# Experts of a mixture: gate and up products with the tokens as the stationary operand, weights split and read unit by unit, modulated rows stored

## The chip, the core and the metric

One core of a Trainium2 chip runs the whole program. The metric is the device time of one execution in microseconds; lower is better. TensorE (PE, its weight loads PEld), VectorE (DVE), ScalarE (ACT), GpSimd (POOL) and SyncE (SP, which here only issues DMAs) run their own instruction queues in order and wait for one another on semaphores.

## What is computed

Two blocks of two layers each on 1024 tokens of width 1024, in float32. The first block (gated delta rule and gated linear attention) is not touched. Each layer of the second block is attention, a residual layer norm, a modulation, a mixture of 32 experts of which each token takes 2, and another residual layer norm:

```python
x = layer_norm_2(DEEPNORM_ALPHA_2 * x + (1 + g1) * y, ln_g[i, 0], ln_b[i, 0])
h = x * (1 + sc2) + sh2
y = hierarchical_moe(h, ...)
x = layer_norm_2(DEEPNORM_ALPHA_2 * x + (1 + g2) * y, ln_g[i, 1], ln_b[i, 1])
# hierarchical_moe: for each expert e, on the rows routed to it
return (jax.nn.silu(xb @ w_gate[e]) * (xb @ w_up[e])) @ w_down[e]
```

`w_gate[e]` and `w_up[e]` are [1024, 512], `w_down[e]` is [512, 1024]; together 6 MB an expert. With this case's inputs, worked out from the reference, the fullest expert has 109 tokens in the first layer and 145 in the second, where the next has 101.

## The kernel before

SBUF is an arena of 47 units of [128, 1024] float32 (512 KB each); PSUM is eight banks of [128, 512]. The program is written as chains (generators) that emit instructions and yield; `Flow.run` picks the next chain by priority and by rough estimates of the engines' times, so one fixed order of instructions for each engine comes out. Every instruction goes through one helper, so the profile gives line 72 to nearly all; shapes and tiles tell them apart.

A float32 product can be made in two ways. As plain float32, TensorE gets one matmul, which stands in the trace as two instructions. As float32r, `split` (line 441) first makes two halves of 12 significant bits: ScalarE copies the value to the high half, VectorE subtracts it from the value for the low half. Three matmuls then give the product: high by high, high by low, low by high. A float32r matmul is one instruction.

A layer's experts run in `moe_experts` (line 2609), at most two open at a time, each a chain `expert` (line 2536):

- `gather` (line 2600): GpSimd clears a unit and fetches the expert's tokens, up to PLACES = 120 rows, from DRAM by an indirect DMA; two experts ahead.
- `turn` (line 564): TensorE turns the rows into eight [128, 120] columns; ScalarE and VectorE take four each out of PSUM, and multiply and shift them by the modulation (`cols`) on the way.
- gate and up: for each of four blocks f of 128 channels, eight plain float32 matmuls with a [128, 128] piece of the weight stationary and the 120 tokens moving. The result has channels on partitions, as the down product needs it.
- ScalarE's silu, VectorE's product and a split; then down: 24 float32r matmuls, the 120 tokens stationary and the weight's halves moving, 512 wide, for two halves n of the width; each half times gate and gain on VectorE, then GpSimd adds the rows to Y in DRAM by an indirect DMA. The last expert's outcome is kept back instead (`hold`).

`Experts` (line 2475) loads the weights ahead on SP, matrix by matrix, each as four units: at most `limit` = 2 matrices at first, 5 later. Gate and up units are read as two pieces of 2 KB for each partition, down units as one of 4 KB. The chain `split` makes the halves of the down matrix's four units; a matrix's units are given back together, at its end.

An expert with more than PLACES tokens gets further blocks in `moe_extra` (line 2666), a loop on the device before the others, in which `Direct` loads the weights for the block; nothing else runs beside it. One such block runs here, in the second layer.

Ahead of the experts, `out_proj_ln` (line 1518) makes the attention's output product tile by tile (eight of 128 tokens). Each tile is normalised in `post` of `moe_front` (line 2293), which also makes the router's logits; `Rows.put` (class at line 1471) then multiplies by ALPHA times gain and adds ALPHA times bias, both on VectorE, and writes the result twice, to x_mid, from which the experts gather, and to Y, to which they add. After the last two tiles `route` counts places; the gathers wait for it. In this stage `Rows.tile` also puts two GpSimd operations of [128, 1024] on each tile that comes in.

Of the kernel before, what the change touches and what calls it, by code (L numbers as in the profile page):

```python
# [30 lines left out]
# Each chain is a generator that emits instructions and yields where its next TensorE work has to wait. Rough  # L31
# estimates of the engines' times say which chain goes on: the first in priority that would not hold TensorE up.
# [27 lines left out]


class Engine:
    """An engine's instructions, each with its estimated time added to the flow's clocks."""
# [51 lines left out]
class Flow:  # L115
# [15 lines left out]
    def ready(self, eng, outs, ins):  # L131
        """When what an instruction reads and writes may be there."""
# [14 lines left out]
    def lag(self, a, b):  # L147
        """From an instruction's end on engine a to the start of one on b that waits for it."""
# [12 lines left out]
    def last(self, ap):  # L161
        """When an access was last used."""
# [20 lines left out]
    def dma(self, out, in_, after=None):  # L183
        """Returns the time by which it may have arrived; after: an instruction that is to end before."""
# [28 lines left out]
    def rank(self, done, prio):  # L213
        """Another priority for a chain, given what spawn() returned."""
# [38 lines left out]
class Buf:  # L253
    """A unit of an arena, or a run of them."""
# [19 lines left out]
class User:  # L274
    """Who takes units: at most peak at a time. Units that earlier users may still need are kept for them."""
# [5 lines left out]
class Arena:  # L281
    """Units of one size; make(i, n, dt) gives the access to n of them from i on, a tensor of its own if fresh."""
# [34 lines left out]
    def now(self, n=1, dt=F32, user=None):  # L317
        """Units that are sure to be free."""
# [30 lines left out]
def rep(ap, n):  # L349
    """A [P, x] access seen as [P, n, x], the same for each n."""  # L350
# [3 lines left out]
def spread(ap, n):  # L354
    """A [P, c] access seen as [P, c, n], each value n times."""
# [3 lines left out]
def rows_of(vec, off, n):  # L359
    """A DRAM vector's n elements from off, for each of 128 partitions."""  # L360
# [55 lines left out]
def sm(K, n):  # L416
    """Room for n values per partition."""
# [3 lines left out]
def rsqrt(K, out, x, n):  # L421
    """out = x ** -0.5 on VectorE: a bit-level first guess and three Newton steps. x, out: [128, n]"""
# [18 lines left out]
def split(K, hi, lo, src, scale=None, pool=False):  # L441
    """src = hi + lo exactly, each with the 12 significant bits of float32r; scale: a power of two. """
# [10 lines left out]
class Weights:  # L453
    """Requests (source, units, scale): DRAM [128, units * 1024] accesses; each comes as (hi, lo) buffers."""
# [5 lines left out]
    def ask(self, srcs, shape, scale=None):  # L460
        """srcs: the unit's DRAM accesses, each with the part of the unit (a function of its view) that it fills."""
# [43 lines left out]
def ask_cols(K, w, col, scale=None):  # L505
    """128 columns of a [D, n] weight as [128, 8, 128]."""
# [4 lines left out]
class XT:  # L511
    """A transposed activation in two float32r halves: hi[k], lo[k] [128, S]; ready[t] per tile of 128 tokens."""
# [6 lines left out]
    def take(self, user=None):  # L519
        """Its units, taken by the first who asks."""  # L520
# [21 lines left out]
def gemm_cols(K, X, w, h):  # L542
    """[128 columns of w, 512 tokens] in a bank, three float32r passes."""
# [20 lines left out]
def turn(K, dst, src, cols=None):  # L564
    """dst, src: [128, 8, 128] accesses; dst[:, c] = transposed src[:, c]; cols [128, 16]: a bias and a scale for each c."""
# [49 lines left out]
def columns(K, vecs):  # L615
    """DRAM vectors of D values as columns [128, (vector, k)]."""
# [15 lines left out]
def affine(K, g, b, out, ready, mod=None, n=0):  # L632
    """Columns (bias | scale) of x g + b, or of that times (1 + sc) + sh: columns n + 1 and n of a layer's modulation."""
# [16 lines left out]
def hybrid_params(K, l):  # L650
    """What a layer needs besides its large weights."""
# [25 lines left out]
    # half of the weights: silu(2 y) = y (1 + tanh(y))  # L677
# [22 lines left out]
def softplus_neg(K, out_ln, x):  # L700
    """out_ln = log(1 + exp(-|x|)); x in SBUF."""
# [19 lines left out]
def small_projections(K, P, X, user):  # L721
    """beta, the decays of the delta rule and the log gates of the linear attention."""
# [41 lines left out]
    # as two float32r parts  # L764
# [4 lines left out]
    # log gates: [128 tokens, 8 chunks, 256]  # L769
# [22 lines left out]
def conv_silu(K, P, X, chunk, user, ev):  # L792
    """silu(causal depthwise convolution) of 128 projected channels: [128, S]."""
# [28 lines left out]
def proj(K, X, user, ev, gate=False, scale=1.0):  # L822
    """128 projected channels [128, S]; gate: 2 silu of them."""
# [21 lines left out]
def proj_rows(K, X, user, ev):  # L845
    """256 projected channels of tokens: [128 tokens, 4, 256] twice."""
# [13 lines left out]
class Out:  # L860
    """128 channels of the heads' outcome: [128, S], to DRAM, or for the last ones as two float32r halves."""
# [19 lines left out]
def head_out(K, o, ss, z, gain, dst, user, by=None):  # L881
    """rms norm of o [128 tokens, 8, 128] per token (ss: sums of squares), its gain, times z [128 channels, S]; to DRAM."""
# [23 lines left out]
def chunks_of(d, c0, n):  # L906
    """n chunks from c0, [128, n, 128], in a DRAM tile where a chunk and the blocks on its diagonal keep one distance."""
# [3 lines left out]
def blocks_of(d, c0, n):  # L911
    """The 16 x 16 blocks on the diagonals of n chunks from c0, [8 n, 16, 16]."""
# [3 lines left out]
def solve(K, H, b, kT, g2, sL, D, L, W):  # L916
    """Half b's transposed T = (I + strict(s k k^T . decay))^-1: blocks of 16 by substitution, then merged in twos."""
# [81 lines left out]
def solve_blocks(K, H, W, g2, user):  # L999
    """The inverses of the 64 blocks I + N of 16 x 16, a partition each, a column of N at a time."""  # L1000
# [18 lines left out]
def norms(K, x, ss, r, user):  # L1019
    """Of [128 tokens, 8, 128]: r = 1 / its rows' lengths."""  # L1020
# [9 lines left out]
def delta_head(K, P, l, h, evs, user, prio, dst):  # L1030
    """Keys and queries stay as they are: their lengths go into the factors of the small matrices and of the outcome."""
# [131 lines left out]
    # the outcome's factors: the queries' ones inside of the norm  # L1163
# [8 lines left out]
def gla_level(K, n, q, k, B, user):  # L1172
    """exp of the decays to a middle place of each 2^(n+1) tokens, times k before it and q after it."""
# [14 lines left out]
def head_sums(K, x):  # L1188
    """Of x [128 = 2 heads x 64, S]: the sums over a head's channels, [128 tokens, (head, 8)]."""
# [11 lines left out]
def gla_pair(K, P, l, pr, evs, user, prio, dsts):  # L1201
# [14 lines left out]
    # both heads' sums over their channels  # L1216
# [65 lines left out]
    # neighbours  # L1282
# [17 lines left out]
    # through the state  # L1300
# [62 lines left out]
def hybrid_layer(K, l, P, X, outs, prio):  # L1363
    """Projections, delta rule and linear attention; the gated heads to outs."""
# [45 lines left out]
def load_rows(K, user, vec):  # L1410
    """A DRAM vector of D values on all partitions."""
# [5 lines left out]
def load_wout(K, w, X, user, out, X2, gain=None):  # L1417
    """A [D, D] weight, its columns times 1 + gain, as out[k] = (hi, lo) [128, D], once X is free; then room is kept for X2."""
# [1491 lines left out]
```

## Time and profile before

| | |
|---|---|
| time, three runs | 4336.83, 4337.46, 4349.83 us; median 4337.46 |
| the profiled execution | span 4333.8 us from the first to the last instruction; 3.7 us less than the median run's time |
| PE busy | 4128.3 us, 95% |
| DVE / ACT / POOL busy | 2642.8 / 1778.6 / 818.2 us |
| DMA | 680.59 MB, 157 GB/s on the mean |
| experts of the first layer | about 2055 to 2728 us of the span |
| experts of the second layer | about 3611 to 4284 us, behind the extra block at 3552 to 3606 us |

The page's second part shows the span in 40 slices, a digit for tenths of a slice's time. A table of stretches gives, for each stretch, the busy time of each engine with its number of instructions, the granted TensorE clock as a share of full speed, the mean busy share of the 16 DMA engines and what they moved. A group of instructions lists those of one shape: count, busy time, mean duration of one, idle time before them and who ended it. PE's matmuls overlap in the pipeline: the mean duration of one is longer than the distance from one start to the next, which sets the rate.

### The profile page before, as it was taken

How to read it: one execution, taken by the hardware profiler on the slowest of the kernel's cores; microseconds unless marked ns; L12 is line 12 of the kernel's file. 1: busy time of each engine (PE TensorE's matmuls, PEld its weight loads, DVE VectorE, ACT ScalarE, POOL GpSimd, SP SyncE). 2: the span in 40 equal slices, each digit the busy share in tenths (PEclk: the TensorE clock that was granted, in tenths of full speed). 3: DMA queues.
4: the chain of work that ended last, by engine and by line, in shares of the span. 5: the costliest groups of instructions: out<-in, count | busy, mean ns of one | idle time of the engine just before them, and what ended most of it. 6: DMA issues, size and time to landing. Idle time of an engine off the chain costs nothing. (4 is left out here: it accounts for less than half of the span.)

```text
span 4333.8 us, 71282 instructions
## 1 busy us (share of the span) xinstructions
PE 4128.3 (95%) x28070; PEld 3462.6 (80%) x28070; DVE 2642.8 (61%) x5593; ACT 1778.6 (41%) x3541; POOL 818.2 (19%) x600
## 2 busy tenths in 40 slices
PE   8999899999999999987999999899999978999997
PEld 6878787888887777766999999776776768999995
DVE  7778767776767766586443444656666674444445
ACT  4333335332334444431333333667777513333331
POOL 1111101211213222241122221300010211222212
PEclk9999899999999999988999999999999989999998
DMA  4323232111134333234999997300010357999994
GB/s 150 85 84 95 79 101 82 49 43 51 41 100 142 117 109 109 81 129 176 323 327 328 326 328 259 112 13 18 20 66 20 112 177 245 324 322 328 335 329 146
DMA packets 404775, 680.59 MB, mean 157 GB/s; under 512 B 59893, under 2 KB 190639, under 8 KB 404437
## 3 DMA queue, kind: packets, MB, share of 16 engines
q1 hardware_dynamic: 386004, 642.85, 43.0%
q0 software_dynamic: 18432, 33.15, 3.4%
q8 instruction: 223, 3.65, 0.3%
q14 instruction: 116, 0.94, 0.1%
HBM read 621.66 MB, written 84.02 MB: 163 GB/s over the span
## 5 line engine op out<-in xcount | busy, mean ns | idle before, releaser
L72 PE MATMUL banks<-slot 128*128 128x120 f32 (+7 forms) x23848 | 3659.8, 317 | 31.5 <-ACT slot L72 13.0
L72 PEld LDWEIGHTS banks<-slot 128*128 128x128 f32 (+4 forms) x23848 | 2982.1, 181 | 585.6 <-issue 213.5
L72 DVE TENSOR_TENSOR slot<-slot 128x1024 fp32r<-128x1024 f32 (+15 forms) x1027 | 851.1, 844 | 452.1 <-ACT slot L72 396.0
L72 ACT ACTIVATE slot<-slot 128x1024 fp32r<-128x1024 f32 (+9 forms) x621 | 579.4, 938 | 817.3 <-DMA slot<-in_moe_w_down 363.2
L72 ACT ACTIVATE slot<-banks 128x512 f32<-128x512 f32 (+8 forms) x929 | 444.6, 491 | 750.8 <-PE banks L72 713.9
L72 POOL TENSOR_TENSOR slot<-slot 128x384 f32<-128x384 f32 (+2 forms) x232 | 343.3, 1501 | 1376.3 <-DVE slot L72 344.8
L72 PE MATMUL banks<-c,slot 128*128 128x128 f32 (+4 forms) x3224 | 477.4, 284 | 90.6 <-DVE slot L72 29.7
L72 PEld LDWEIGHTS banks<-c,slot 128*128 128x128 f32 (+3 forms) x3224 | 383.1, 150 | 167.7 <-issue 58.7
L72 ACT ACTIVATE slot<-banks,small 128x120 f32<-128x120 f32 (+1 forms) x400 | 262.7, 682 | 472.0 <-PE banks L72 399.9
L72 DVE TENSOR_TENSOR slot<-slot,banks 128x512 f32<-128x512 f32 (+3 forms) x175 | 114.5, 660 | 475.0 <-PE banks L72 261.2
L72 ACT ACTIVATE slot<-slot,small 128x1024 f32<-128x1024 f32 (+1 forms) x292 | 266.4, 922 | 237.9 <-DVE small L72 231.4
L72 DVE COPY slot<-banks 128x512 f32<-128x512 f32 (+7 forms) x406 | 221.4, 551 | 129.8 <-PE banks L72 99.2
L72 POOL MEMSET slot<- 120x1024 f32 (+2 forms) x70 | 66.4, 954 | 1066.3 <-PE banks L72 847.6
L72 DVE TENSOR_REDUCE small<-banks 128x1 f32<-128x1024 f32 x128 | 156.2, 1223 | 104.5 <-PE banks L72 104.5
L72 POOL DMA_INDIRECT Y<-slot,small x62 | 139.3, 2246 | 261.9 <-DVE slot L72 260.4
L72 DVE TENSOR_TENSOR slot<-banks,slot 64x512 fp32r<-64x512 f32 (+3 forms) x257 | 123.8, 497 | 64.4 <-ACT slot L72 54.3
L72 DVE SCALAR_TENSOR_TENSOR small<-small 128x1 f32<-128x1 f32 (+3 forms) x590 | 131.9, 230 | 12.5
L72 DVE SCALAR_TENSOR_TENSOR slot<-slot,c_act 128x1024 f32<-128x1024 f32 x84 | 119.5, 1424 | 24.8 <-DMA slot<-in_ada_w 24.1
L72 PE MATMUL banks<-small,slot 128*128 128x128 f32 (+1 forms) x576 | 104.5, 296 | 24.1 <-DVE small L72 19.7
L72 PEld LDWEIGHTS banks<-small,slot 128*128 128x128 f32 (+1 forms) x576 | 81.9, 196 | 39.7 <-issue 17.0
L72 DVE SCALAR_TENSOR_TENSOR slot<-banks,cw,slot 128x511 f32<-128x511 f32 (+1 forms) x144 | 106.8, 745 | 6.1 <-ACT slot L72 4.1
L72 DVE SCALAR_TENSOR_TENSOR slot<-banks,small,slot 120x512 f32<-120x512 f32 x128 | 95.4, 745 | 23.3 <-PE banks L72 23.3
(133 smaller groups left out, 1715.1 us busy)
## 6 DMA issues: line engine op xcount, KB each, us to landing
slot<-in_moe_w_down SPq DMA_DIRECT2D x260, 512.0 KB
slot<-in_moe_w_gate SPq DMA_DIRECT2D x260, 512.0 KB
slot<-in_moe_w_up SPq DMA_DIRECT2D x260, 512.0 KB
slot<-in_ada_w SPq DMA_DIRECT2D x96, 512.0 KB
slot<-in_w_in SPq DMA_DIRECT2D x56, 512.0 KB
xb<-slot SPq DMA_DIRECT2D x40, 512.0 KB
slot<-xb SPq DMA_DIRECT2D x24, 512.0 KB
slot<-in_na_w_qkv SPq DMA_DIRECT2D x24, 512.0 KB
```

The source lines that it names most:

```text
L72: r = real(*a, **k)
```

## The change

PLACES becomes 128. Gate and up are turned round: the tokens' columns are stationary ([128, 128] for each of eight pieces k of the depth) and the weight moves, 512 wide. Each unit of gate and up now holds two rows of the weight for each partition, which lie side by side in DRAM, so it is read in one 4 KB piece; the columns of x are picked in the same order (every second one). Of the eight gate and up units of an expert, the first of each matrix stays plain float32 (`PLAIN`); the other six, and down's four, are split, up to six units ahead of their use (`SPLIT`). Units are loaded, counted (`limit` 8, 20, 22 units) and given back one by one. The tokens' columns are split as well. The product's result has tokens on partitions and takes four more transposes ahead of down. Down's two halves run side by side, a unit at a time.

The modulation leaves the expert: `Rows.prepare` makes two more rows on all partitions from gain, bias and modulation (one VectorE and three GpSimd operations of [128, 1024]), and `put` makes the modulated rows with them on VectorE, for x_mid, ahead of the residual rows for Y, whose two operations go from VectorE to GpSimd. Room kept for this stage goes from 37 to 39 units. Comments and docstrings are removed throughout.

```diff
-PLACES = 120  # of an expert, in one go
+PLACES = 128
+PLAIN = (0, 4)
+SPLIT = 6
+def units_of(w, i):
+    return w.rearrange("o (n p j) f -> p (o n) (j f)", n=4, j=2 if i < 2 else 1)
 class Experts:
     def load(self):
...
-                w = K.I[name][self.l][e].rearrange("(k p) f -> p k f", p=128)
-                b, t = yield from load_matrix(K, i, lambda k, n: w[:, k:k + n, :], self.user)
+                w = units_of(K.I[EXPERT_W[u // 4]][self.l][e:e + 1], u // 4)
+                b = yield from K.A.take(self.user)
+                t = K.F.dma(b.f, w[:, u % 4])
+                if u in PLAIN:
+                    K.F.set(self.there[e][u], (b,), t)
                 else:
-                    self.raw.append((b, t))
+                    self.raw.append((e, u, b, t))
     def split(self):
...
+            while not self.raw or self.ahead >= SPLIT:
+                yield lambda: self.raw and self.ahead < SPLIT
+            e, u, b, t = self.raw.pop(0)
+            self.ahead += 1
             yield from K.F.until(t)
+            w = yield from self.halves(b)
+            K.F.set(self.there[e][u], w)
 def expert(...):
-    xT = yield from A.take()
-    turn(K, xT.rows()[:, :, :c], x.rows()[:c], cols)
+    xh, xl = yield from several(A, 2, None, F32R)
+    xf = sm(K, 2 * c)
+    xv = x.f[:c].rearrange("p (n c j) -> p n j c", n=4, j=2)
+    for g in range(2):
+        p = yield from K.banks.take()
+        for j in range(4):
+            T.transpose(p.f[:, j * c:(j + 1) * c], xv[:, 2 * g + j // 2, j % 2], K.ident[:c, :c])
+        if not g:
+            F.scalar.activation(xf.f[:, 0:2 * c], p.f[:, 0:2 * c], AF.Copy)
+        o, m = (0, 4 * c) if g else (2 * c, 2 * c)
+        split(K, xh.r[:, 4 * g * c + o:4 * g * c + o + m], xl.r[:, 4 * g * c + o:4 * g * c + o + m], p.f[:, o:o + m])
...
-        for f in range(4):
-            for k in range(KD):
-                T.matmul(p.f[:, f * c:(f + 1) * c], wv[k // 2][:, k % 2, f * 128:(f + 1) * 128], xT.rows()[:, k, :c],
-                         start=(k == 0), stop=(k == KD - 1))
+        for n in range(4):
+            w = yield from get.next(i, n)
+            for j in range(2):
+                k, s = 2 * n + j, slice(512 * j, 512 * j + 512)
+                if len(w) == 1:
+                    T.matmul(p.f[:c], xf.f[:, j * c:(j + 1) * c], w[0].f[:, s], start=(k == 0), stop=(k == KD - 1))
+                else:
+                    cut = slice(k * c, (k + 1) * c)
+                    product(p.f[:c], xh.r[:, cut], xl.r[:, cut], w, s, k == 0, k == KD - 1)
+            get.done(w)
             yield
...
+    for f in range(4):
+        T.transpose(p.f[:, f * c:(f + 1) * c], a.f[:c, f * 128:(f + 1) * 128], K.ident[:c, :c])
 class Rows:
     def prepare(self, K, user, write=False):
+        if self.mod is not None:
...
+            K.F.vector.tensor_scalar(sc.f, sc.f, 1.0 / ALPHA, 1.0 / ALPHA, op0=ALU.mult, op1=ALU.add)
+            P.tensor_mul(g.f, self.rows[0].f, sc.f)
+            P.tensor_mul(sc.f, self.rows[1].f, sc.f)
+            P.tensor_add(sc.f, sc.f, sh.f)
-    def put(self, K, x, t):
+    def put(self, K, x, t, user):
+            h = yield from K.A.take(user)
+                V.tensor_mul(h.f, x.f, self.rows[2].f)
+                V.tensor_add(h.f, h.f, self.rows[3].f)
+                K.F.dma(self.also[t * 128:(t + 1) * 128, :], h.f)
             if self.early:
-                self.affine(K, x, 2)
+                self.affine(K, x)
-        freed.limit = 5
+        freed.limit = 20
-        W.limit = 5
+        W.limit = 22
```

## Rows read from the trace of the kernel before

**Rows 1.** page, busy tenths in 40 slices of 108 us

```profile
PE   8999899999999999987999999899999978999997
DVE  7778767776767766586443444656666674444445
DMA  4323232111134333234999997300010357999994
```

**Rows 2.** stretch: length, PE, PEld, DVE, ACT, POOL busy, PEclk, DMA, GB/s

```profile
4000.00:4100.00 100.00, 99.85 (x760) 92.80 (x760) 39.47 (x57) 32.10 (x48) 20.16 (x14) 1.00 0.97 332
```

**Rows 3.** chain that ended last, second layer: start, us, what

```profile
3649.13 20.90 PE banks L72 x160
...
4214.59 20.92 PE banks L72 x160
```

**Rows 4.** PE groups, 2302.4 to 2323.3 us: count, busy, mean ns, idle

```profile
L72 PE MATMUL banks<-slot 128*128 128x120 f32 x128 | 15.1, 275 | 0.0
L72 PE MATMUL banks<-slot 128*120 128x512 f32 x24 | 6.3, 403 | 0.0
L72 PE MATMUL banks<-c,slot 120*128 120x120 f32 x8 | 1.1, 266 | 0.0
```

**Rows 5.** PE group of 1983 to 1990 us; two timeline rows

```profile
L72 PE MATMUL banks<-slot 128*128 128x512 f32 x31 | 7.3, 393 | 0.0
...
2728.34 1.88 PE L72 MATMUL banks<-slot,c 128*128 128x512 f32 x4
...
1979.36 1.03 PE L72 MATMUL banks<-c,slot 128*128 128x128 f32 x8
```

**Rows 6.** table of stretches inside one expert's period

```profile
2329.00:2334.00 5.00, 5.00 (x35) 4.48 (x34) 0.79 (x1) 1.66 (x2) 2.05 (x2) 1.00 1.02 418
2334.00:2336.00 2.00, 2.00 (x20) 2.00 (x19) 2.00 (x3) 1.63 (x3) 0.00 (x0) 1.00 1.04 395
2316.00:2320.00 4.00, 4.00 (x39) 4.00 (x38) 2.09 (x2) 0.51 (x1) 2.31 (x1) 1.00 1.01 253
2322.00:2325.00 3.00, 2.97 (x25) 2.65 (x24) 2.21 (x5) 2.04 (x5) 0.00 (x0) 1.00 1.01 322
2325.00:2327.00 2.00, 2.00 (x17) 1.85 (x16) 0.51 (x2) 0.00 (x0) 0.00 (x0) 1.00 0.59 226
```

**Rows 7.** groups by shape, DVE and ACT, 2300 to 2321 us

```profile
L72 DVE TENSOR_TENSOR slot<-slot 128x1024 fp32r<-128x1024 f32 x4 | 4.8, 1219 | 7.6 <-ACT slot L72 7.6
L72 DVE TENSOR_SCALAR slot<-banks,small 128x120 f32<-128x120 f32 x4 | 1.5, 400 | 0.0
L72 DVE SCALAR_TENSOR_TENSOR slot<-banks,small,slot 120x512 f32<-120x512 f32 x2 | 1.5, 745 | 0.0
L72 DVE TENSOR_TENSOR slot<-slot,banks 128x480 f32<-128x480 f32 x1 | 0.7, 655 | 5.2 <-PE banks L72 5.2
...
L72 ACT ACTIVATE slot<-slot 128x1024 fp32r<-128x1024 f32 x4 | 4.2, 1058 | 7.7 <-DMA slot<-in_moe_w_down 7.5 <-ACT slot L72 0.2
L72 ACT ACTIVATE slot<-banks 128x480 f32<-128x480 f32 x1 | 0.6, 571 | 0.1
```

**Rows 8.** timeline, the first layer's norm tiles: start, us, operation, count

```profile
1914.75 16.57 POOL L72 TENSOR_TENSOR slot<-slot 128x1024 f32<-128x1024 f32 x6 [0.19 <-DMA slot<-xb]
...
1924.36 7.17 DVE L72 SCALAR_TENSOR_TENSOR small<-small 128x1 f32<-128x1 f32 x4
...
1942.01 1.50 DVE L72 SCALAR_TENSOR_TENSOR small<-small 128x1 f32<-128x1 f32 x7
```

**Rows 9.** timeline, PE: router's wait; products of the extra block

```profile
2035.20 0.18 PE L72 MATMUL banks<-both,before_b 128*128 128x32 bf16 x1 [8.59 <-DVE both L72]
...
3573.29 16.76 PE L72 MATMUL banks<-slot 128*128 128x120 f32 x126 [1.50 <-DMA slot<-in_moe_w_up]
...
3591.43 5.83 PE L72 MATMUL banks<-slot 128*120 128x512 f32 x24 [1.38 <-ACT slot L72]
```

**Rows 10.** group of the whole run: GpSimd on [128, 1024]

```profile
L72 POOL TENSOR_TENSOR slot<-slot 128x1024 f32<-128x1024 f32 x76 | 182.4, 2403 | 661.1 <-DMA slot<-xb 322.5 <-ACT slot L72 201.9 <-DVE slot L72 91.4
```

More of the change, by code (lines that the diff above doesn't have):

```diff
@@ L1556, in finish @@
         if not after.early:
-            after.put(K, x, t)
+            yield from after.put(K, x, t, user)
         yield
@@ L1560, in finish @@
         if after.early:
-            after.put(K, x, t)
+            yield from after.put(K, x, t, user)
         A.give(x)
@@ L2326, in moe_front @@
     K.banks.give(p)
[L2327 to L2328 removed]
+    K.small.give(c)
     M.there = [Event() for _ in range(NT)]
@@ L2479, in __init__ @@
         self.K, self.l = K, l
-        self.limit, self.out, self.go = 2, 0, Event()
-        self.raw, self.there = [], [[Event() for _ in range(3)] for _ in range(32)]
+        self.limit, self.out, self.ahead, self.go = 8, 0, 0, Event()
+        self.raw, self.there = [], [[Event() for _ in range(12)] for _ in range(32)]
         self.user = K.A.user(5000, 0)
@@ L2486, in load @@
         for e in range(32):
-            for i, (name, kk, n) in enumerate(EXPERT_W):
+            for u in range(12):
                 while self.out >= self.limit:
@@ L2533, in done, with expert @@
         self.out -= 1
-def expert(K, get, tok, gate, gn, cols, rows, Y, x=None, hold=None):
+        if len(bufs) > 1:
+            self.ahead -= 1
+def expert(K, get, tok, gate, gn, rows, Y, x=None, hold=None):
     F, T, V, A = K.F, K.F.tensor, K.F.vector, K.A
@@ L2574, in expert @@
         F.set(hold.near)
+    yield
+    ps = [(yield from K.banks.take()), (yield from K.banks.take())]
+    for f in range(4):
+        w = yield from get.next(2, f)
+        for n in range(2):
+            product(ps[n].f[:c], hh[:, f], hl[:, f], w, slice(n * 512, n * 512 + 512), f == 0, f == 3)
+        get.done(w)
+        if f < 3:
+            yield
     for n in range(2):
         s = slice(n * 512, n * 512 + 512)
-        p = bank(K)
-        for f in range(4):
-            yield
-            T.matmul(p.f[:c], hh[:, f], w[f][0].r[:, s], start=(f == 0), stop=False)
-            T.matmul(p.f[:c], hh[:, f], w[f][1].r[:, s], start=False, stop=False)
-            T.matmul(p.f[:c], hl[:, f], w[f][0].r[:, s], start=False, stop=(f == 3))
-        with F.aside() if n == 0 else ExitStack():
-            V.scalar_tensor_tensor(y.f[:c, s], p.f[:c], gate[:c], gn.f[:c, s], op0=ALU.mult, op1=ALU.mult)
-            K.banks.give(p)
-            if hold is not None:
-                split(K, h[0].r[:c, s], h[1].r[:c, s], y.f[:c, s])
-                F.set(hold.half[n], h)
-    get.done([b for hl in w for b in hl])
+        V.scalar_tensor_tensor(y.f[:c, s], ps[n].f[:c], gate[:c], gn.f[:c, s], op0=ALU.mult, op1=ALU.mult)
+        K.banks.give(ps[n])
+        if hold is not None:
+            split(K, h[0].r[:c, s], h[1].r[:c, s], y.f[:c, s])
+            F.set(hold.half[n], h)
     A.give(hs)
@@ L2606, in gather, with moe_experts @@
     return x
-def moe_experts(K, l, W, R, gn, cols, rows, Y, prio, first, hold, there):
+def moe_experts(K, l, W, R, gn, rows, Y, prio, first, hold, there):
     F = K.F
@@ L2715, in moe_extra @@
         block()
-        for _ in expert(K, Direct(K, l, e), tok, gate[:, 2:3], gn, cols, rows, Y):
+        for _ in expert(K, Direct(K, l, e), tok, gate[:, 2:3], gn, rows, Y):
             pass
@@ L2811, in moe_layer @@
     ln = F.spawn(moe_ln(K, l, Y, last_one.rrows(), hold, there, x_out, N, user, prio + 200), prio + 200)
-    yield from moe_experts(K, l, W, R, gn, M.cols.f, rows.x, Y, prio + 110, first, hold, there)
-    K.small.give(M.cols)
+    yield from moe_experts(K, l, W, R, gn, rows, Y, prio + 110, first, hold, there)
     K.small.give(R.small)
```

109 lines of the change are left out of this document (54 added, 55 removed).

## The prediction

> **What bounds the kernel now.** I read the slices first: where the experts run at their steady pace (slices 20 to 24 and 35 to 39) PE and DMA show nines, and VectorE threes and fours [rows 1]. So two resources are candidates there, and the table of one such stretch says how close they are: PE is busy 99.85 of 100 us at full clock, and the DMA engines 0.97 at 332 GB/s [rows 2]. The chain of waits decides between them. In the second layer it is PE on itself: 28 rows of 160 matmuls each, one per expert, with starts from 3649.13 to 4214.59, which is 27 periods of 20.94 us, and no wait for data between them [rows 3]. PE sets the pace, and the DMA engines, with 0.97 x 20.94 = 20.3 us of work in each period, are only 0.6 us behind. A cure for PE alone would be worth little; the change touches both.
>
> What PE does in a period is 128 instructions of 120 columns for gate and up (64 matmuls of two), 24 of 512 columns for down and 8 transposes, 160 in all [rows 4]. The 128 take some 14.6 of the 20.94 us: a load of 128 stationary columns is paid for only 120 moving ones.
>
> **The change part by part. PE.** Rates at full clock first. 31 float32r matmuls of 512 columns took 7.3 us with a mean duration of 0.39; (7.3 - 0.39) / 30 is a distance of 0.230 us, so the last one's end stands out by 0.16. Four plain float32 instructions of 512 columns took 1.88, so (1.88 - 0.16) / 4 = 0.43 each; eight transposes 1.03, so 0.109 each [rows 5]. After the change an expert has four plain pieces of the depth (two units of two), 4 x 2 x 0.43 = 3.44; twelve split ones, 12 x 3 x 0.230 = 8.28; down, 24 x 0.230 = 5.52; transposes, 12 x 0.109 = 1.31. The sum is 18.55 us against 20.94. The strided stationary operand of the eight transposes of x is not in this trace; its cost lies between nothing and 0.11 each (as much again as a transpose), 0.9 an expert. I take nothing, since it is off the bound below.
>
> **DMA.** The bytes stay: 332 GB/s x 20.94 us = 6.95 MB an expert, of which 12 x 512 KB = 6.29 are weights. Only the pieces change, 2 KB to 4 KB for two thirds of them. Down's 4 KB pieces move at 418 GB/s with the engines full, a stretch nearly all of 2 KB pieces at 395 [rows 6]. That is 6%, far less than a halved count of pieces suggests. Two phases of each period are slower although the engines are just as full: 253 GB/s for 4 us behind the scatter to Y, 322 for 3 us during the gather [rows 6]. I keep both phases as they are, since their slowness comes with the rows that are added and fetched, and put the rest at 418: 4 us for 1.01 MB, 3 us for 0.97 MB, and 4.97 MB / 418 = 11.9 us. The sum is 18.9 us. From below the bound is 6.95 / 418 = 16.6 (the slow phases gone). From above it is 19.7: today's two microseconds at a share of 0.59 [rows 6], where a transfer waits for units, come on top with 0.8. I take 19.1, near the middle sum, because units now come back one by one. So **DMA would set the pace, at 19.1 us**, half a microsecond over PE's sum.
>
> **Splits.** ScalarE and VectorE now make the halves of ten units instead of four. VectorE: ten subtractions of 1.22 are 12.2; x's halves 0.66 and about half of it; the product 0.66; the split ahead of down 0.66; two gated outcomes 1.49; in all 16.0 us. The 1.5 us of modulations go. ScalarE: ten copies of 1.06 and five smaller ones of up to 0.57, some 13 us [rows 7]. Both lie beside PE and fit into 19.1 us, VectorE with 84%. If that cover goes they are the bound (third rival).
>
> Sum of the steady part: 62 periods (64 experts, less the first of each layer) x (19.1 - 20.94) = **-114 us**.
>
> **Ahead of the experts.** For each tile two VectorE operations are replaced by two others of the same shape, and two of 2.4 us go to GpSimd [rows 10]: 16 in each layer. For the first six tiles PE's products cover them. The last two tiles have no cover: PE waits 8.59 us for the router's chain on VectorE [rows 9], and GpSimd's four operations, 9.6 us, now run beside that chain. What that does the trace shows: beside six GpSimd operations (1914.75 to 1931.3) four tiny VectorE operations of [128, 1] took 7.17 us; seven of them took 1.50 with GpSimd idle [rows 8]. So between 0 and 9.6 us a layer; I take 5, as the router's operations are many and some fall between. In `prepare`, three GpSimd operations and one of VectorE (1.2) do the same while attention ends: 0 to 8.4 a layer, I take 2, since other chains give PE work there. Together +14 for both layers. The Trainium skill, SBUF — State Buffer (SBUF: two separate sides), states an exclusive lock: a VectorE operation with two SBUF inputs waits for a whole GpSimd operation that reads SBUF. This trace's 7.17 us agree; by the rule in full these terms would be +36 instead of +14 and the time 4261.
>
> The modulated rows are written ahead of the residual ones, so the gathers don't wait longer; Y is due only at the first scatter, some 40 us later: nothing. SP issues as many weight DMAs as before, one per unit: nothing.
>
> **Edges.** At a layer's start PE can begin with the plain unit, but the next units need splits of 1.2 us each, which at four already ran there: 0 to 3 us, I take 1 a layer. At the end the last expert's extra transposes (0.4) and their copy stand alone: 0 to 2, I take 1. The extra block of the second layer is serial: its products take 16.76 + 5.83 = 22.6 us [rows 9], and 18.6 after; but up to four splits come ahead of PE's use: -5 to +5, I take -2. Together +2.
>
> Sum: -114 + 14 + 2 = -98 us on the profiled span of 4333.8, so 4235.8. That span lies 3.7 us below the median of the three runs, which takes the same difference: **4239 us**.
>
> **The rivals.** *PE's floor is reached.* If the two slow DMA phases shrink with the larger pieces, PE's 18.55 sets the pace: 62 x (18.55 - 20.94) = -148, +16, 4205 us. For it: only 2 KB pieces run in those phases today, so nothing shows how 4 KB ones fare. Against it: the rate of full engines differs by 6% only. The Trainium skill, Perfetto Trace Analysis (DMA Optimizations), says that batching from 2 KB to 4 KB can dramatically improve throughput; that would end here, and this trace's 395 against 418 GB/s don't bear it out.
>
> *The larger pieces gain nothing.* Then the DMA work stays 20.3 us a period: 62 x (20.3 - 20.94) = -40, +16, 4314 us. The row of 418 GB/s speaks against it.
>
> *VectorE's queue sets the pace.* Its queue is in order, and six of its operations for an expert wait for PE (x's two, the product, down's split, two outcomes); the splits of coming units stand behind them. Today that shows as 5.2 us of idle time ahead of the product [rows 7], harmless at 40% load. With 16.0 us of work, waits of 4.2 us a period give 20.2 us and 4337 - 46 + 16 = 4308. Up to six units split ahead, some 8 us of PE work, speak against it.
>
> *Slower, by the same queue.* From waits of 4.9 us on, the period exceeds today's. If each of the six operations waits 1 us, it is 22.0: 62 x 1.06 = +66, +16, 4419 us. For it: one such wait alone is 5.2 today. Against it: such a wait costs PE nothing while units split ahead last, and the change lets six be ahead.
>
> **How the numbers follow.** Forecast, DMA at 19.1: 0.45. PE's floor: 0.20. VectorE's queue at 20.2: 0.15. Pieces without gain: 0.07. Slower by the queue: 0.09. All within 13 us of today, a mixture of these: 0.04. The range takes the first three: its low end is PE's floor with the extra block's best case and the other terms at nothing (-148 - 5), 4184; its high end is the queue's 4308, rounded to 4310. A measurement of this kernel can tell about 0.3%, 13 us: faster 0.45 + 0.20 + 0.15 + 0.07 = 0.87, same 0.04, slower 0.09.
>
> **What would show it.** Right: periods of about 19 us between the scatters to Y, PE with short idle times put down to DMA or to the splits' halves, a DMA share of 0.97 or more at some 365 GB/s (6.95 MB / 19.1), VectorE at 80 to 87%. PE without idle time and a period of 18.6 is the first rival; PE waiting for VectorE with a DMA share under 0.93 is the queue. The router's wait of 8.59 us growing to 12 or more would show GpSimd's operations beside it. The prediction is wrong if the slow DMA phases change their length with the larger pieces, or if VectorE waits longer for PE than the splits ahead cover.

## The result and the profile after

The changed kernel takes 4623.72 us (median of six runs, 4616.56 to 4643.76) where the kernel before took 4340.91: a ratio of 1.0656, 95% interval 1.0633 to 1.068. It is 6.6% slower; the forecast was 2.3% faster.

The profiled execution took 4643.76 us, the longest of the six, with a span of 4641.8 us, 308 more than before. The slices of its page answer to [rows 1]:

```profile
PE   8999999999999999778878789899999868888787
DVE  7778767757676665776656566665576766565667
PEclk9999899999999999778988989999999878989888
DMA  4333241112242332348777776100022267777774
```

Where the experts run (slices 19 to 24 and 34 to 39) PE shows sevens and eights and DMA sevens (one eight), where both had nines, and the granted clock shows more eights than nines, where it had nines nearly throughout. No resource is full any more. A stretch of each kernel, before and then after, as in [rows 2] (length; PE, PEld, DVE, ACT, POOL busy; PEclk; DMA share; GB/s), says the same:

```profile
2200.00:2600.00 400.00, 399.45 (x3056) 372.31 (x3055) 164.71 (x228) 129.78 (x190) 85.24 (x57) 1.00 0.96 329
...
2200.00:2600.00 400.00, 321.83 (x1227) 236.34 (x1228) 240.33 (x249) 190.87 (x236) 66.34 (x45) 0.89 0.76 262
```

The scatters to Y mark the experts and divide the span. Between the starts of the first and the 31st of a layer lie 752.9 and 748.7 us, where 626.4 and 626.0 lay before: +249 us in 60 distances (25.0 instead of 20.9 on the mean; the median is 26.0, since the first and the last of a layer are shorter). From the first bn aggregate of the normalisation stage to the first scatter (in the second layer to the extra block's) the two layers took 370.8 us instead of 325.2: +46. The stretch from the extra block's scatter to the first of the second layer's experts and the tail behind the last scatter are 4 us shorter together. The other 17 us lie ahead of the change, in code that is the same in both (last section). 249 + 46 - 4 + 17 = 308.

What an expert waits for shows in one period. These are timeline rows of after (start, us, engine, operation, count; in brackets the idle time before and what ended it):

```profile
2396.47 1.59 POOL L72 DMA_INDIRECT Y<-slot,small  x1 [0.16 <-DVE slot L72]
...
2405.91 1.23 DVE L72 TENSOR_TENSOR slot<-slot 128x1024 fp32r<-128x1024 f32 x1 [6.59 <-DMA Y<-slot,small]
2407.17 2.00 ACT L72 ACTIVATE slot<-slot 128x1024 fp32r<-128x1024 f32 x2 [8.29 <-DVE slot L72]
...
2410.14 1.12 PE L72 MATMUL banks<-c,slot 128*128 128x128 f32 x4 [5.13 <-DVE slot L72]
...
2411.04 3.62 PE L72 MATMUL banks<-slot,small 128*128 128x512 f32 x4
```

GpSimd starts the scatter at 2396.47. A subtraction that makes a weight's low half is to write into the very unit that the scatter still reads, so VectorE stands for 6.59 us until the scatter lands; the subtraction starts 9.4 us after the scatter. The profile leaves buffer numbers out, so which unit an instruction takes is inferred from who waits for whom; two experiments below put it to the test. Behind it on VectorE's queue stands the product of gate and up; ScalarE waits for VectorE, then PE 5.13 us for that product. PE's clock has dropped when it goes on after these 5.13 us: the granted clock of the next 5 us is 0.50, its lower level, and the four plain float32 instructions take 3.62 us, in [rows 5] 1.88.

```profile
2410.00:2415.00 5.00, 4.87 (x10) 2.70 (x11) 3.97 (x6) 3.91 (x6) 0.00 (x0) 0.50 0.14 57
```

The waits of after from 2200 to 2600 us (who waited for what: us in total, times, longest) put 11 of some 15 periods down to the scatter, and five waits to weights that come late:

```profile
ACT slot L72 <- DVE slot L72: 171.4, 76, 8.8
...
PE banks L72 <- DVE slot L72: 81.3, 16, 5.6
DVE slot L72 <- DMA Y<-slot,small: 72.6, 11, 6.8
...
DVE slot L72 <- DMA slot<-in_moe_w_up: 27.1, 5, 7.1
```

Ahead of the experts the router's row, as in [rows 9], has grown:

```profile
2070.94 0.19 PE L72 MATMUL banks<-both,before_b 128*128 128x32 bf16 x1 [12.77 <-DVE both L72]
```

### The profile page after: what moved, and what is told of

Its sections match the earlier page's. It is cut to its first block, busy times and chain, and to the rows that moved or that the text cites. A ratio compares the mean times of both kernels' runs of the same rounds, so it can differ in the third digit from the quotient of the medians.

```text
span 4641.8 us, 62336 instructions
## 1 busy us (share of the span) xinstructions
PE 4132.4 (89%) x22870; PEld 3207.2 (69%) x22870; DVE 3122.0 (67%) x5851; ACT 2131.4 (46%) x3866; POOL 924.6 (20%) x638
## 5 line engine op out<-in xcount | busy, mean ns | idle before, releaser
L72 PE MATMUL banks<-slot 128*128 128x512 f32 (+8 forms) x17868 | 3356.4, 352 | 41.9 <-DVE slot L72 18.2
L72 PEld LDWEIGHTS banks<-slot 128*128 128x128 f32 (+4 forms) x17868 | 2532.7, 180 | 739.1 <-issue 293.0
L72 DVE TENSOR_TENSOR slot<-slot 128x1024 fp32r<-128x1024 f32 (+14 forms) x1352 | 1316.9, 984 | 674.7 <-DMA Y<-slot,small 265.1
L72 ACT ACTIVATE slot<-slot 128x1024 fp32r<-128x1024 f32 (+5 forms) x946 | 926.8, 1009 | 1132.2 <-DVE slot L72 779.2
L72 PE MATMUL banks<-c,slot 128*128 128x128 f32 (+2 forms) x3484 | 544.8, 296 | 369.8 <-DVE slot L72 303.6
L72 PEld LDWEIGHTS banks<-c,slot 128*128 128x128 f32 (+1 forms) x3484 | 439.9, 163 | 468.1 <-DVE slot L72 313.8
L72 POOL TENSOR_TENSOR slot<-slot 128x384 f32<-128x384 f32 (+3 forms) x270 | 449.1, 1683 | 1433.8 <-DVE slot L72 407.7
L72 PE MATMUL banks<-slot,small 128*128 128x512 f32 (+2 forms) x648 | 353.9, 686 | 16.3 <-ACT small L72 8.6
L72 DVE TENSOR_TENSOR slot<-banks,slot 128x512 fp32r<-128x512 f32 (+6 forms) x452 | 229.3, 538 | 74.5 <-ACT slot L72 63.7
L72 ACT ACTIVATE slot<-banks,small 128x1024 f32<-128x1024 f32 x140 | 156.2, 1117 | 73.3 <-DVE small L72 72.8
```

Of the source, the lines that this page charges most:

```text
L72: r = real(*a, **k)
```

## The experiments

**The unit of the outcome.** The theory: when the planner gives the outcome y back, it takes the scatter to end 4.04 us after its start (1.04 in `pool_cost` and 3.0 in `Engine`), so that a split gets a unit that is still being read. One line tells it a later time (13.04; the expectations call a unit a slot):

```diff
+    F.mark("POOL", F.last(y.f) + 9.0, [], [y.f])
     A.give(y)
```

> The changed kernel with one line added: the planner is told that the slot of an expert's outcome y comes free 9 us later than it had assumed, so that it gives other slots to the next splits; nothing else of the computation or of the queues is edited. Theory (the slot): in the changed kernel one split subtraction on VectorE waits up to 7.4 us per expert for the scatter that still reads its slot, and the product of gate and up and PE stand behind it. Then this wait is gone, the distance between scatters falls from 26.3 us to 18.5 to 20.5 us, and the time falls by 62 x (26.3 - 19.5) = some 360 to 480 us less what DMA then holds up: 4180 to 4350 us. Rival (VectorE's queue by itself: its operations wait for PE's results, whichever slots they use): the distance stays at 25 us or more and the time above 4540 us. Rival (weights arrive late): the same 25 us or more, with VectorE waiting for the weights' transfers instead of the scatter.

4304.59 us, ratio 0.992 (0.9891 to 0.9949): 319 us from one line. The distance is 19.30, constant to 0.03 in the middle of the first layer, and VectorE waits neither for a scatter nor for `in_moe_w_up` any more: the late weights came of the same stall.

```profile
2200.00:2600.00 400.00, 390.14 (x1660) 292.55 (x1659) 310.77 (x332) 256.30 (x312) 92.41 (x61) 1.00 0.98 354
```

PE is at full clock, so the clock of 0.89 in after was a consequence of the stalls. PE was busy for 321.83 / 400 x 26.0 = 20.9 us a period there, with 5.1 idle; here for 18.8 with 0.5 idle. Of the 6.7 us between the periods 4.6 are idle time and 2.1 the clock.

The other way to take the wait away is to take the reader of the unit away.

```diff
-    F.gpsimd.indirect_dma_start(out=Y, ..., compute_op=ALU.add)
```

> The changed kernel without the scatters of the experts' outcomes (the rows are not added; nothing else is edited, the planner is not told of another time). Theory (the slot): a slot that no scatter reads has nothing to wait for, so the distance between the gathers falls from 26.3 us to 18.7 to 19.5 us, as with the slot's correction. Rival (the correction helped because it dealt the slots out in another order): the distance stays above 23 us. What it falls below 19.3 is the scatter's own price on the DMA engines.

The distance between gathers is 19.1 us. Two quite different edits, a later time in the planner and no scatter at all, take the same 7 us away; without the scatter an expert is only 0.2 us shorter than with the later time.

A smaller dose:

```diff
+    F.mark("POOL", F.last(y.f) + 2.0, [], [y.f])
```

> The changed kernel with a smaller dose of the slot's correction: the planner takes the outcome's slot to be free 2 us later than it had assumed (6 us after the scatter's start instead of 4), where the scatter lands 9.3 us after its start (median of the changed kernel). Theory (the slot): the slot goes to a split that VectorE reaches about 2 us later, so the wait of 6.6 us per expert shrinks to 4 to 5 us and the distance between scatters to 23 to 24.5 us, between the 26.1 without and the 19.3 with 9 us. Rival (any other order of the slots would have cured it): 19.3 us. Rival (the wait has another cause): 26 us.

4252.27 us, a distance of 18.55: not the part of the gain that I expected (a period of 23 to 24.5 us), but more than all of it. The same kernel once more:

> The kernel with the slot declared free 2 us later once more, timed: its one run was 4252 us beside 4340 for the kernel before. In that run a weight load, not a split, took the outcome's slot, so SyncE's queue waits for the scatter and VectorE does not, and PE was busy without a gap at 18.55 us an expert, the sum that my prediction had for PE. I expect 4235 to 4265 us, a ratio of 0.975 to 0.985.

4248.98 us, ratio 0.9789 (0.977 to 0.9808). Stretch and PE timeline:

```profile
2200.00:2600.00 400.00, 400.00 (x1728) 306.42 (x1727) 329.90 (x345) 261.72 (x325) 90.89 (x63) 1.00 0.98 365
```

```profile
2353.06 1.89 PE L72 MATMUL banks<-slot,small 128*128 128x512 f32 x4
2354.39 10.15 PE L72 MATMUL banks<-slot 128*128 128x512 f32 x42
2364.38 1.88 PE L72 MATMUL banks<-slot,small 128*128 128x512 f32 x4
2365.70 4.66 PE L72 MATMUL banks<-slot 128*128 128x512 f32 x18
2370.20 1.60 PE L72 MATMUL banks<-c,slot 128*128 128x128 f32 x12
2371.63 1.89 PE L72 MATMUL banks<-slot,small 128*128 128x512 f32 x4
```

PE has no gap. Why two microseconds were enough the waits of SyncE's queue say, from 2200 to 2600 us. The kernel before:

```profile
SPq L185 <- DMA Y<-slot,small: 121.2, 20, 6.7
```

After:

```profile
SPq L185 <- PE banks L72: 334.4, 177, 10.4
```

With the dose of 2 us:

```profile
SPq L185 <- DMA Y<-slot,small: 65.5, 11, 7.3
```

As far as these waits tell, what counts is who takes the unit next, not by how much the time is off. In the kernel before a weight load took it, and SyncE waited 20 times for the scatter, up to 6.7 us, while PE was busy for 399.45 of 400 us. After the change units come and go one by one and a split takes it; SyncE no longer waits for a scatter, and VectorE does. Two microseconds later in the planner's book a weight load takes it again, in half of the periods at least (11 waits in some 21; 19 in the first run). With 9 us neither SyncE nor VectorE waits for a scatter, so whoever takes the unit takes it after the landing; which one that is, the waits don't show. The instructions come in another order, and a period is 0.75 us longer than with 2 us, 0.47 of it PE's idle time for ScalarE's copy of x, as PE's timeline with the dose of 9 us shows:

```profile
2353.28 1.88 PE L72 MATMUL banks<-slot,small 128*128 128x512 f32 x4
2354.60 4.66 PE L72 MATMUL banks<-slot 128*128 128x512 f32 x18
2359.10 1.11 PE L72 MATMUL banks<-c,slot 128*128 128x128 f32 x8
2360.68 1.13 PE L72 MATMUL banks<-slot,small 128*128 128x512 f32 x2 [0.47 <-ACT small L72]
```

**GpSimd ahead of the experts.**

```diff
             if self.early:
-                self.affine(K, x)
+                self.affine(K, x, 2)
```

> The changed kernel with the residual rows' two operations per tile put back from GpSimd to VectorE (VectorE then does four per tile, GpSimd none in the normalisation's second half). The stage ahead of the experts was 63 us longer than before in both layers together. Theory (GpSimd's operations stretch VectorE's: two-input operations of 1024 took 3.0 us beside GpSimd and 1.2 alone): the stage gets 30 to 60 us shorter although VectorE has 16 operations of 1.2 us more per layer (19 us), so 4565 to 4595 us. Rival (the time there went to the modulated rows' own operations, slots and transfers): within 15 us of the changed kernel's 4624, or above it by up to 30 us. The experts' distance stays 26 us by both.

4612.07 us, ratio 1.0612 (1.0565 to 1.0658). The two stages took 348.2 us instead of 370.8: 22.6 less, under my 30 to 60; the median fell by 12 only. (The 63 us of the expectation are these 46 and the 17 ahead of the change.) Together with the unit's correction:

> Both edits together: the outcome's slot declared free 9 us later, and the residual rows' operations back on VectorE. If the two losses are independent (the slot's in the experts, GpSimd's ahead of them), the gains add to within 15 us: with the theories' values 4125 to 4310 us, faster than the kernel before (4340). If VectorE's queue or late weights are the cause in the experts, it stays above 4500 us.

4276.16 us, ratio 0.9856 (0.9813 to 0.9899). The stages took 345.3 us, with the correction alone 368.2: again 22.9. So the two losses are independent. VectorE's operations of this shape from the first layer's first aggregate to its first gather (count, busy us, mean ns, idle before), in the kernel before, after, and with both edits:

```profile
L72 DVE TENSOR_TENSOR slot<-slot 128x1024 f32<-128x1024 f32 x16 | 19.6, 1222 | 3.9 <-ACT slot L72 3.7
```

```profile
L72 DVE TENSOR_TENSOR slot<-slot 128x1024 f32<-128x1024 f32 x16 | 27.1, 1711 | 0.8 <-ACT slot L72 0.7
```

```profile
L72 DVE TENSOR_TENSOR slot<-slot 128x1024 f32<-128x1024 f32 x32 | 37.6, 1215 | 0.0
```

Sixteen operations took 7.5 us more beside GpSimd's. Twice as many with GpSimd quiet took 1215 ns each. In the second layer the mean grew from 1368 to 2060 ns, and both edits bring it to 1215 there too.

**The modulated rows.** The unit's correction, and the rows undone:

```diff
-    mid = Rows(Y, ..., early=True, also=x_mid, mod=mod)
+    mid = Rows(x_mid, ..., early=True, also=Y)
+    cols = sm(K, 16); F.spawn(load_cols(K, cols, mod), prio + 69)
...
+            if k % 2:
+                V.tensor_scalar(dst, src, cols[:, 8 + k:9 + k], cols[:, k:k + 1], op0=ALU.mult, op1=ALU.add)
+            else:
+                F.scalar.activation(dst, src, AF.Identity, bias=cols[:, k:k + 1], scale=cols[:, 8 + k:9 + k])
```

> The changed kernel with the slot's correction, and with the modulated rows undone: the residual rows are written unmodulated to both places as before, by VectorE, and x is modulated at each expert between its transposes and its halves (four small operations on VectorE and four on ScalarE for an expert, as before; the plain piece of x comes out of these and its own copy goes). Theory (what is left ahead of the experts is the modulated rows' price: their operations on GpSimd and VectorE and their second buffer): the first scatter comes at 2083 to 2090 us and the gap to the extra block's scatter is 885 to 895 us, as before, where the kernel with the slot's correction alone has 2121.5 and 907.3; the experts' distance stays 19.3 us if PE is their bound, up to 20 us if VectorE's 1 us more counts. Together 4230 to 4280 us. Rival (the stage ahead is longer because loads and splits of the many smaller units stand in its queues, not because of the rows): the first scatter stays at 2110 us or later, 4290 us or more.

4231.93 us, ratio 0.9749 (0.972 to 0.9778), the best of the kernels that leave nothing out. The stages took 164.0 and 164.4 us, before 160.1 and 165.1: the price of the rows is gone. The first scatter, at 2111.0, did not come where I expected it, because the stage began at 1947.1 in this execution and at 1923.1 in that of before, behind identical code. The distance is 18.7 us with PE at 398.21 of 400 us: the 1 us more on VectorE (88%) costs no more than 0.1 to 0.2 us over the 18.55 of the dose of 2 us. Of the 46 us of the stages, then, 23 are those of the residual rows on GpSimd, 17 to 20 the modulated rows' own operations, `prepare`'s included (345.3 or 348.2 less 328.4), and 3 remain.

**What DMA needs.** The first test was the 4 KB pieces alone, in the kernel before:

```diff
-                w = ...[e].rearrange("(k p) f -> p k f", p=128)
+                w = ...[e:e + 1].rearrange("o (m p j) f -> p (o m) (j f)", m=4, j=2)
...
```

> The kernel before with one part of the change alone: gate and up are read in pieces of 4 KB (the layout of the changed kernel); products, splits and rows as before. It leaves the matching rearrangement of x out, so each weight row meets another element of x than it should; shapes and counts are the same. By the terms of my sum the DMA work of an expert falls from 20.3 to 18.9 us, PE stays the bound at 20.9: the time stays within 0.5% of before, and the DMA share of a steady stretch falls from 0.97 to 0.89 to 0.93. If larger pieces gain nothing, the share stays at 0.96 or more; if they gain what halved counts of pieces suggest, it falls under 0.85.

4342.41 us, ratio 0.9999 (0.9977 to 1.002). The DMA share between 2200 and 2600 us went from 0.96 to 0.93 (from 4000 to 4100 from 0.97 to 0.95), the smallest fall that I expected, or less. A share beside a full PE does not say what DMA could do, so PE had to be made faster. First without the third pass of gate and up:

```diff
-        T.matmul(o, lo, w[0].r[:, s], start=False, stop=last)
+        if third:
+            T.matmul(o, lo, w[0].r[:, s], start=False, stop=last)
...
```

> The changed kernel with the slot's correction, gate and up without their third pass (the low half of x by the high half of the weights is left out, 12 matmuls of 512 columns an expert), everything else as it is: PE has 12 x 0.23 = 2.8 us less work in a period of 19.3. It asks for the floor of DMA, which my prediction put at 19.1 us. If DMA's work is what its share says (0.985 x 19.3 = 19.0 us), the distance between scatters stays at 18.9 to 19.1 us and the DMA share goes to 0.99. If DMA's slow phases are elastic, it falls to 16.5 (PE), or to 17 to 18 us where VectorE with 15.2 us of work and its waits comes first.

Distance 18.26 us on the mean of a layer, DMA share 0.99 at 365 GB/s, under the 18.9 that the share had promised. The same with 2 KB pieces:

```diff
-    return w.rearrange("o (n p j) f -> p (o n) (j f)", n=4, j=2 if i < 2 else 1)
+    return w.rearrange("o (n j p) f -> p (o n) j f", n=4, j=2 if i < 2 else 1)
...
```

> The kernel without the third pass of gate and up (PE has 2.8 us less work, so DMA sets the pace: 18.26 us an expert at a share of 0.99), but with gate and up read in pieces of 2 KB as before the change: two pieces per partition and unit, x's columns transposed in the matching order. It prices the 4 KB pieces where DMA is the bound. By my prediction's rates (395 GB/s for 2 KB pieces, 418 for 4 KB, two thirds of the bytes) the distance between scatters rises by 3 to 6%, to 18.8 to 19.4 us. By the share that the kernel before showed (0.97 of 20.94) it is 20.3. If pieces of 2 KB cost nothing, it stays at 18.3; if halved pieces would halve the speed, it is over 22.

18.28. An equality this close need not come from DMA: PE and VectorE wait for each other in both kernels (PE's loads for VectorE 52.2 and 51.0 us in 400). So the last two, the second of them with 2 KB pieces, go further: gate and up keep one pass of three, and six of the ten subtractions of an expert go from VectorE.

```diff
-            w = yield from self.halves(b)
+            w = yield from self.halves(b, u < 8)
...
-        T.matmul(o, hi, w[0].r[:, s], start=first, stop=False)
-        T.matmul(o, hi, w[1].r[:, s], start=False, stop=False)
-        T.matmul(o, lo, w[0].r[:, s], start=False, stop=last)
+        T.matmul(o, hi, w[0].r[:, s], start=first, stop=last and not third)
+        if third:
...
```

> To uncover DMA's floor, PE and VectorE are taken far out of its way: gate and up keep one pass of three (the low halves of x and of the weights are left out there, and the ten minus four subtractions of VectorE that make the weights' low halves go); weights are loaded as in the changed kernel, 4 KB pieces, with the slot's correction. PE's work is 13 us an expert, VectorE's some 8. If the 418 GB/s of full engines hold for all 6.95 MB of an expert, the distance between scatters falls to 16.6 us; if the slow phases at the scatter and the gather stay as I priced them, to 18.9; if the 18.26 us of the kernel without the third pass were DMA's floor, it stays at 18.3.

> The same with gate and up read in pieces of 2 KB. By my rates the distance is 3 to 6% over that of the 4 KB pieces; by the DMA share of the kernel before taken as work it is 20.3 us; if the size of the pieces does not count between 2 and 4 KB, it is the same within 0.1 us, as it was with the third pass alone left out (18.28 and 18.26).

17.74 and 18.06 us on the mean of a layer's 30 distances. But such a mean is too low for DMA's work: the first four distances are 10.4 to 15.7 us, of experts whose weights had been loaded ahead. From the ninth scatter of a layer to the 29th the two take 18.6 and 18.9 us an expert (means of both layers), and without the third pass 18.6 and 18.7. Their stretches, 4 KB first:

```profile
2200.00:2600.00 400.00, 337.28 (x1208) 207.56 (x1207) 186.69 (x217) 268.28 (x326) 74.73 (x62) 0.96 0.99 368
```

```profile
2200.00:2600.00 400.00, 335.67 (x1184) 204.54 (x1184) 183.57 (x212) 262.93 (x321) 73.15 (x61) 0.94 1.00 362
```

DMA is full in both; PE is at 84% and VectorE at 47%. DMA needs 18.6 us an expert with 4 KB pieces and 18.9 with 2 KB: under 2%, and 368 against 362 GB/s say the same, where I had 6% from the rates and 20.3 us from the share. (Each kernel ran once.) The kernel with the dose of 2 us, with all its passes, takes 18.5 us in the same stretch: PE and DMA are level there, and a faster PE alone gains nothing.

## Why the prediction was wrong, step by step

**PE's sum: right.** 18.55 us was forecast; with the outcome's unit out of the way PE does 18.57, without a gap. By kind: plain float32 2 x 1.32 = 2.6 (forecast 3.44), float32r 9.99 + 4.50 = 14.5 (13.80), transposes 1.44 (1.31). The distances of [rows 5] erred by -0.8, +0.7 and +0.1, and the errors cancelled: that the sum came out to 0.02 us is luck.

**DMA as the pace, 19.1 us: half a microsecond too much, and no longer the pace.** DMA needs 18.6 us, level with PE's 18.57; the prediction's own middle sum of 18.9 was nearer than the 19.1 it took. What was wrong lies behind it. The prediction took 0.97 x 20.94 = 20.3 us as work [rows 2, 3]. It was not: in a kernel that asks for more, the same 2 KB pieces need 18.9. DMA engines beside a slower PE are busy longer for the same bytes. The rates inside a period [rows 6] were no rates of the pieces either: 6% became 2%. The Trainium skill, Perfetto Trace Analysis (DMA Optimizations), says that batching small transfers, from 2 KB to 4 KB, can dramatically improve throughput; for pieces of these sizes within transfers of 512 KB it made under 2% here. The rival *PE's floor is reached* had the right bound, with DMA just as near; its place was taken by something else.

**Units given back one by one: the step that failed.** The prediction put this edit at nothing, even at a gain ("because units now come back one by one"), and asked of the splits only whether VectorE has time. It never asked which unit a split writes into, and who still reads it. VectorE's work was as forecast (240.33 of 400 us in a period of 26.0 is 15.6 us; 16.0 forecast). The rivals *VectorE's queue sets the pace* and *slower, by the same queue* had the right place, an in-order queue with coming splits behind a stalled operation, and the sign that was named for them came (PE waiting for VectorE, DMA share under 0.93). But the wait is for a DMA, not for PE: I had priced six waits for PE of 1 us each, a period of 22.0; it is one wait of 6.6, and 26. A row that warned of it stood in the trace of before, and the prediction made nothing of it: SyncE's 121.2 us for `Y<-slot,small`. A wait on a queue that costs nothing names a unit that comes free late; the question is who will take it when the order of the units changes.

**Ahead of the experts, +14: too small by a factor of three.** It is +46. The router's wait of 8.59 us [rows 9] became 12.77, as the sign said (12 or more), but in the second layer 8.52 became only 9.57: most of the loss lies elsewhere. The starts of the tiles' bn aggregates show where. Up to the sixth tile's the first layer lost 8 us and the second none (-1.5); from the sixth to the eighth they took 37.6 and 54.9 us instead of 31.4 and 31.1, +30 together; behind the eighth +9. So "for the first six tiles PE's products cover them" was wrong: in the second layer VectorE had made 4 of its 16 operations on the rows ahead of the sixth aggregate, in the kernel before 10. They were put off, not covered, and came in front of the last tiles, beside GpSimd's, as these lines of that layer show (VectorE's, then GpSimd's):

```profile
3689.01 1.22 DVE L72 TENSOR_TENSOR slot<-slot 128x1024 f32<-128x1024 f32 x1
...
3690.74 3.02 DVE L72 TENSOR_TENSOR slot<-slot 128x1024 f32<-128x1024 f32 x1
...
3690.30 5.71 POOL L72 TENSOR_TENSOR slot<-slot 128x1024 f32<-128x1024 f32 x2 [1.50 <-DVE slot L72]
```

VectorE was busy for 112.9 of 140 us in the first layer's stage, before for 91.1 of 121. Since the rows of [rows 8] already showed such stretching, the cover was the mistake more than the price. That the 23 us of GpSimd's rows come from this stretching alone is not shown, since the edit that moves them changes the order of all instructions there too. The Trainium skill, SBUF — State Buffer (SBUF: two separate sides), states an exclusive lock between a GpSimd operation and a VectorE operation with two SBUF inputs; by it the term would have been +36, nearer than my +14. VectorE's 1711 ns beside GpSimd against 1215 without agree with it in direction; GpSimd's share of the measured loss is 23 us.

**Edges, +2: small, as forecast, but of the other sign.** The extra block took 27.7 us from its first transposes to its scatter, before 29.0 (-2 forecast); from that scatter to the next one 38.2, before 41.3; and the tail is 1 us shorter, where +1 was forecast. (The terms add to +2 only if the one for the end counts for each layer; else to +1.)

With a later time in the planner (the 2 us), the forecast of 4239 us would have come within 10 us of the measured 4249, but partly by luck: the steady part gives -126 (forecast -114), the stages +48 (forecast +14), and shorter stretches elsewhere make up for the rest. PE's 18.57 us in all 62 periods would have been -147; the last distances of a layer are longer (24.5 and 19.8 us).

## What to carry to other kernels

When a change alters how often and in which order buffers are recycled, list for each buffer with a slow reader, above all a scatter, who writes it next, and on which queue: a wait that was free on the queue of the loads costs a third of a period on an engine's in-order queue. A planner's constant for a transfer (4.04 us here, where the landing takes 9.3) decides this silently, so it deserves a check against the trace. The landing time itself was not tried: 6.04 and 13.04 us both took the stall away, and the longer of them, by the order that came of it, was slower by 0.75 us a period. A DMA share of 0.97 beside a full engine is no measure of DMA's work; only a kernel in which that engine is not full shows it (18.9 us here, not 20.3). And a mean over a whole run of experts is shortened by what was loaded ahead.

## What was not expected of the hardware

A scatter of up to 128 rows takes long to land in the stream of weight loads. This is the last line of the view of the scatters of after:

```profile
DMA to landing us min/median/max: 4.8/9.3/11.6
```

The medians of the kernels with the later time are 9.5 (9 us) and 9.1 (2 us); of the kernel before no landing is given. The 4.8 is the extra block's, which has nothing beside it but only 17 tokens in its 128 places, so what the loads cost is not shown.

The code of the first block, far ahead of the change, took some 15 us more in the profiled execution of after than in that of before. By the same instructions of PE in both, 5 of them are there by 910 us, and some 8 more arise about here, between 910 and 960 us (before, then after; columns as above):

```profile
930.00:950.00 20.00, 19.12 (x183) 17.74 (x183) 19.36 (x44) 5.62 (x13) 0.90 (x1) 1.00 0.29 79
```

```profile
930.00:950.00 20.00, 19.58 (x156) 17.31 (x157) 12.92 (x25) 7.29 (x18) 3.76 (x2) 0.51 0.13 32
```

PE ran at half its clock (1.2 of 2.4 GHz) in one and at full clock in the other, in the same code. In after it had stood for 2.08 us for VectorE just before, in before for 0.75. It is not the kernel alone that decides: the two runs with the dose of 2 us are one kernel, and their granted clocks here are 1.00 and 0.55. Over all runs the stage ahead of the experts starts 1922.5 to 1947.1 us into the span, of this one kernel at 1928.5 and 1938.6. What decides it is open. So two profiles of one program can differ by 10 us in places that no edit touched, and the terms above were compared stage by stage.
